# HGRN mixing with the tokens divided by two in seven levels instead of by four in three and a half

## The chip, the cores and the metric

The kernel runs on one core of a Trainium2 chip. The metric is the device time of one execution in microseconds (us). Before the change the median of three runs is 2312.23 us (2312.05 to 2313.69).

## What is computed

The model is a two-layer trunk on 256 tokens of width 2048, all in float32. Layer 0 mixes tokens with HGRN2, a gated linear recurrence with 16 heads of key width 128; layer 1 with a causal gate (gMLP). Each is followed by a gated ConvFFN, and each of the four steps ends in a residual and a layer norm. The change concerns the token mixing of HGRN2 alone:

```python
proj = x @ w_in
q, f, i, g = jnp.split(proj, ...)
q = silu(q); v = i
log_forget = logaddexp(log(lb), log1p(-lb) + log_sigmoid(f))
k = (1.0 - lb) * sigmoid(-f)
...
cum = jnp.cumsum(lf_c, axis=2)
rel = cum[:, :, :, None, :] - cum[:, :, None, :, :]
decay = jnp.exp(jnp.where(mask[:, :, None], rel, -jnp.inf))
scores = jnp.einsum('bhtk,bhsk,bhtsk->bhts', q_c, k_c, decay)
out = (jnp.einsum('bhts,bhsv->bhtv', scores, v_c) + ...)   # plus the carried state
...
o = o * rsqrt(mean(o * o) + RMS_EPS) * norm_g * silu(g)
return o @ w_out
```

The score of a later token t with an earlier token s is a sum over the key width of q[t] * k[s] * (product of the forget gates after s up to t).

## The kernel before

**Weights.** All weights arrive from HBM in chunks of 512 x 512 (1 MB, SyncE's queue, `fetch`). `convert` splits each into two float32r parts: `whi` by a copy on ScalarE (line 83), `wlo` by a subtraction on VectorE (line 84), in two halves. At most three chunks are held ahead.

**Products.** `block_b` (lines 149 and 156) has the weights stationary and makes an output of 512 features x 256 tokens; `block_a` (lines 113 to 115) has the activations stationary. Both feed TensorE with two float32r parts, three products for each exact one.

**HGRN.** `hgrn` runs four groups of four heads. A group is `block_b` for q, `block_b` for f, `block_a` for v, then two calls of `mix` (two heads each), then `block_b` for the gate `sg`, whose result is needed only after the mixing. The code is unrolled, and a scheduler places the instructions of each engine's queue when the program is built: what comes first in the program has priority, and what is ready earlier may be put ahead. On TensorE, products of the `sg` block are thus placed among those of `mix`. An engine takes its own queue strictly in that order.

**The mixing of two heads** (`mix`). The key feature is on the partition; `q`, `f`, `k1` hold 2 heads x 256 tokens = 512 elements a partition. For each head and each half of 128 tokens (index `th`, four of them; `own(th)` is its slice) the scores [s, t] are a 128 x 128 tile. They are collected in `sc`, and after that multiplied with `v`. The steps:

- `Q = q * f` (line 524); `pd`: four products of `k` and `q`, whose diagonals go to `sc` by a predicated copy (528 to 530).
- Three levels with b = 1, 4, 16 (lines 531 to 573). The tokens are divided in groups of four segments of b. `K` carries the gates from s to the end of its segment, `Q` those from the start of t's segment, `T` the product of a whole segment. For a pair of segments at distance 1, 2 or 3 the gates of the segments between are missing, so a tile `W` of 192 columns for each `th` holds three versions of `Q`: a copy on ScalarE (538) and two multiplications on VectorE (539, 540). Four products `K` x `W` (544) go into two tiles `pl` in PSUM, and six predicated copies (553) with `mask[b]` put the three distances into `sc`. Five small multiplications make `G` and the next `T` (through the helper `mul`, whose instructions all stand at line 559). New `Q` and `K` for segments four times as long come from two copies on ScalarE (567, 570) and four multiplications on VectorE.
- A last level with b = 64, written out: four products of 128 columns (577) and one predicated copy with `upper` (578).
- The cross term between the two halves, `pc` (592), and the output `pout` (600 to 602).

The PSUM tiles of all these (`pd`, `pl`, `pc`, `pout`) share a pool, `misc`, of two slots. `Q`, `K` and `T` have two slots each, `W` and `G` one. `masks` (on GpSimd) builds the masks once at the start.

A float32 product that isn't split (all of those in `mix`) appears in the trace as two passes, each with its own weight load. Matmul records are on the engine PE, weight loads on PEld.

Of the kernel before, what the change touches and what calls it, by code (L numbers as in the profile page):

```python
# [8 lines left out]
F32 = mybir.dt.float32  # L9
F32R = mybir.dt.float32r  # L10
U32 = mybir.dt.uint32
AF = mybir.ActivationFunctionType
ALU = mybir.AluOpType
PSUM = bass.MemoryType.PSUM

P = 128
S = 256
# [11 lines left out]
LEVELS = (1, 4, 16)  # L29
# [6 lines left out]
class Trunk:  # L36
    """Activations that feed products are kept as an exact sum of two float32r parts,
    feature on the partition, [P, k, part, token]; weights are split the same way as
    they arrive, and a product is hi*hi + hi*lo + lo*hi."""
# [21 lines left out]
    # ---------------------------------------------------------------- weights  # L61
# [37 lines left out]
    # ---------------------------------------------------------------- products  # L99
    def block_a(self, act, ka, w, k0, nch, c0, evac, staggered=False, halves=False):  # L100
        """out[token, c0:c0+NB]; act is stationary."""
# [38 lines left out]
    def block_b(self, act, w, nch, c0, evac, halves=False):  # L140
        """out[c0 + feature, token] in four tiles, [P, main | rest, token]; the weights
        are stationary."""
# [47 lines left out]
    def gather(self, pool, ps, out):  # L190
        """out = main + rest of a tile of block_b."""
        nc = self.nc
        r = pool.tile([P, S], F32, tag="rest", name="rest")
        nc.scalar.copy(r, ps[:, 1, :])  # L194
        nc.vector.tensor_tensor(out, ps[:, 0, :], r, ALU.add)

    def split(self, out, k, src):
        """out[:, k] = the two parts of src [P, token]."""
        nc = self.nc
        nc.scalar.copy(out[:, k, 0, :], src)  # L200
        nc.vector.tensor_tensor(
            out[:, k, 1, :], src, out[:, k, 0, :].bitcast(F32), ALU.subtract
        )

    # ---------------------------------------------------------------- constants
# [13 lines left out]
    def load_vectors(self, rows_sb):  # L219
        """Per-feature vectors as columns: feature k*P + p of row r at [p, base + k]."""  # L220
# [50 lines left out]
    def bounds(self, h1):  # L271
        """lb = softmax over the rows of lb_logits, row 0, and 1 - lb."""
# [15 lines left out]
    # ---------------------------------------------------------------- layouts  # L288
    def turn(self, t, k0, n=4, g=None, b=None):
        """X[:, k0 : k0 + n, :, half t] from the columns of z[half t], with x -> g*x + b."""  # L290
# [20 lines left out]
    # ---------------------------------------------------------------- layer norm  # L311
# [15 lines left out]
    def norm(self, name, l, store=None):  # L327
        """Layer norm of z, half by half as its last product arrives. With store, the
        result goes there; without, it goes to X, and z holds it once residual() has run."""
# [43 lines left out]
    def add_z(self, c, first=False, last=False):  # L373
        """evac of block_a: z[:, t, NB columns c] gains the product, the first time as
        ALPHA * z + product."""
        nc = self.nc

        def evac(t, ps):
            with self.tc.high_priority() if last else nullcontext():
                step(t, ps)  # L380

        def step(t, ps):
            zz = self.z[:, t, c * NB : (c + 1) * NB]
            if first:
                nc.vector.scalar_tensor_tensor(zz, zz, ALPHA, ps, ALU.mult, ALU.add)
            else:
                nc.vector.tensor_tensor(zz, zz, ps, ALU.add)  # L387
            if last:
                nc.vector.bn_stats(self.stats[t][:, c, :], zz)
                if c == 3:  # L390
                    self.after_stats(t)

        return evac

    # ---------------------------------------------------------------- HGRN2
# [12 lines left out]
    def masks(self):  # L408
        """mask[b][s, (group, i, r)] = 1 where row s lies in segment i of that group of four
        segments of b rows."""  # L410
        nc, cp = self.nc, self.cp
        self.mask = {}
        for b in LEVELS:
            n = P // 4 // b
            m = cp.tile([P, n, 3, b], F32, name=f"mask{b}")
            nc.gpsimd.memset(m, 1.0)
            nc.gpsimd.affine_select(
                out=m, in_=m, pattern=[[-4 * b, n], [-b, 3], [0, b]], compare_op=ALU.is_ge,
# [3 lines left out]
                out=m, in_=m, pattern=[[4 * b, n], [b, 3], [0, b]], compare_op=ALU.is_ge,  # L422
# [3 lines left out]
        self.upper = cp.tile([P, 1], F32, name="upper")  # L426
        nc.gpsimd.memset(self.upper, 1.0)
        nc.gpsimd.affine_select(
            out=self.upper, in_=self.upper, pattern=[[0, 1]], compare_op=ALU.is_ge,
            fill=0.0, base=P // 2 - 1, channel_multiplier=-1,  # L430
        )
# [82 lines left out]
    def mix(self, q, f, k1, v, sc, o, ss, lp, h1):  # L514
        """Two heads. The decay between s < t is a product of forget gates; it is taken as
        (gates from s to the end of its segment) * (gates of the segments between) *
        (gates from the start of t's segment), at the one level of a division of the tokens
        by four at which s and t part. Q and K carry the outer two."""
        nc = self.nc
        flat = lambda x: x.rearrange("p h n -> p (h n)")  # L520
        own = lambda th: slice((th % 2 * 2 + th // 2) * P, (th % 2 * 2 + th // 2 + 1) * P)
        K, T = flat(k1), flat(f)
        Q = lp.tile([P, 2 * S], F32, tag="Q", name="Q")
        nc.vector.tensor_tensor(Q, flat(q), T, ALU.mult)
# [6 lines left out]
        for b in LEVELS:  # L531
            n = 2 * S // (4 * b)
            seg = lambda x: x.rearrange("p (n i r) -> p n i r", i=4, r=b)
            row = lambda x: x.unsqueeze(3).to_broadcast([*x.shape, b])
            Qv, Kv, Tv = seg(Q), seg(K), T.rearrange("p (n i) -> p n i", i=4)
            W = lp.tile([P, 4, 192], F32, tag="W", name="W", bufs=1)
            Wv = W.rearrange("p x (n i r) -> p (x n) i r", i=6, r=b)
            nc.scalar.copy(Wv[:, :, 0:3, :], Qv[:, :, 1:4, :])
            nc.vector.tensor_tensor(Wv[:, :, 3:5, :], Qv[:, :, 2:4, :], row(Tv[:, :, 1:3]), ALU.mult)
            nc.vector.tensor_tensor(Wv[:, :, 5:6, :], Wv[:, :, 4:5, :], row(Tv[:, :, 1:2]), ALU.mult)  # L540
            for t in range(2):
                pl = self.misc.tile([P, 2, 192], F32, tag="m", name="pl")
                for h in range(2):
                    nc.tensor.matmul(  # L544
                        pl[:, h, :], K[:, own(2 * t + h)], W[:, 2 * h + t, :], start=True, stop=True
                    )
                at = 0
                for d in (1, 2, 3):
                    w = (4 - d) * b
                    dst = sc[:, t].rearrange("p h (n x) -> p h n x", x=4 * b)[:, :, :, d * b :]  # L550
                    src = pl.rearrange("p h (n x) -> p h n x", x=6 * b)[:, :, :, at : at + w]
                    mk = self.mask[b].bitcast(U32)[:, :, 0 : 4 - d, :].rearrange("p n i r -> p n (i r)")
                    nc.vector.copy_predicated(  # L553
                        dst, mk.unsqueeze(1).to_broadcast([P, 2, P // 4 // b, w]), src
                    )
                    at += w
            G = lp.tile([P, P, 4], F32, tag="G", name="G", bufs=1)[:, :n, :]
            Tn = lp.tile([P, P], F32, tag="T", name="T")[:, :n]
            mul = lambda out, x, y: nc.vector.tensor_tensor(out, x, y, ALU.mult)  # L559
            mul(G[:, :, 0], Tv[:, :, 0], Tv[:, :, 1])  # L560
            mul(G[:, :, 1], G[:, :, 0], Tv[:, :, 2])
            mul(G[:, :, 3], Tv[:, :, 2], Tv[:, :, 3])
            mul(G[:, :, 2], G[:, :, 3], Tv[:, :, 1])
            mul(Tn, G[:, :, 0], G[:, :, 3])
            Qn = lp.tile([P, 2 * S], F32, tag="Q", name="Q")
            Kn = lp.tile([P, 2 * S], F32, tag="K", name="K")
            nc.scalar.copy(seg(Qn)[:, :, 0, :], Qv[:, :, 0, :])
            mul(seg(Qn)[:, :, 1:2, :], Qv[:, :, 1:2, :], row(Tv[:, :, 0:1]))
            mul(seg(Qn)[:, :, 2:4, :], Qv[:, :, 2:4, :], row(G[:, :, 0:2]))
            nc.scalar.copy(seg(Kn)[:, :, 3, :], Kv[:, :, 3, :])  # L570
            mul(seg(Kn)[:, :, 2:3, :], Kv[:, :, 2:3, :], row(Tv[:, :, 3:4]))
            mul(seg(Kn)[:, :, 0:2, :], Kv[:, :, 0:2, :], row(G[:, :, 2:4]))
            Q, K, T = Qn, Kn, Tn
        b = P // 2
        pl = self.misc.tile([P, 4, P], F32, tag="m", name="pl")
        for th in range(4):
            nc.tensor.matmul(pl[:, th, :], K[:, own(th)], Q[:, own(th)], start=True, stop=True)  # L577
        nc.vector.copy_predicated(
            scv[:, :, b:], self.upper.bitcast(U32).unsqueeze(2).to_broadcast([P, 4, b]), pl[:, :, b:]
        )  # L580
# [38 lines left out]
    def staggered_pass(self, act, ka, w, k0):  # L619
        """The last CK k-tiles of all four column blocks, half t = 0 first."""  # L620
# [15 lines left out]
    # ---------------------------------------------------------------- gMLP  # L636
# [90 lines left out]
    # ---------------------------------------------------------------- ConvFFN  # L727
# [128 lines left out]
```

## Time and profile before

| what | value |
|---|---|
| device time, median of 3 runs | 2312.23 us |
| span of the profiled execution, first to last instruction | 2310.0 us |
| mean granted TensorE clock | 0.998 |
| VectorE / ScalarE busy, whole span | 1499.2 / 1090.2 us |
| first products of the four groups' mixing (`pd`) at | 83.5, 190.3, 297.2, 404.0 us |
| HBM, read and written | 185 GB/s over the span |

The device time includes what lies around the span. Busy time of an engine counts the stretches in which at least one of its instructions was in flight; TensorE's are pipelined, so a record is longer than the distance between two of them. In a chain of waits, on the other hand, the length of a piece is the time for which it held the end back. The chain of work is followed back from the last instruction, and names for each stretch of time the one engine and line that everything behind it had to wait for.

### The profile page before, as it was taken

How to read it: one execution, taken by the hardware profiler on the slowest of the kernel's cores; microseconds unless marked ns; L12 is line 12 of the kernel's file. 1: busy time of each engine (PE TensorE's matmuls, PEld its weight loads, DVE VectorE, ACT ScalarE, POOL GpSimd, SP SyncE). 2: the span in 40 equal slices, each digit the busy share in tenths (PEclk: the TensorE clock that was granted, in tenths of full speed). 3: DMA queues.
4: the chain of work that ended last, by engine and by line, in shares of the span. 5: the costliest groups of instructions: out<-in, count | busy, mean ns of one | idle time of the engine just before them, and what ended most of it. 6: DMA issues, size and time to landing. Idle time of an engine off the chain costs nothing.

```text
span 2310.0 us, 30477 instructions
## 1 busy us (share of the span) xinstructions
PE 2287.9 (99%) x12141; PEld 1956.5 (85%) x12141; DVE 1499.2 (65%) x2407; ACT 1090.2 (47%) x1642; POOL 43.3 (2%) x86
## 2 busy tenths in 40 slices
PE   8999999999999999999999999999999999999998
PEld 7888888888888888888888888888888888888886
DVE  5868786857765666456665776566765566466656
ACT  5565555536443444334443645445443444344442
POOL 2000000000000000000000000000000000000000
PEclk9999999999999999999999999999999999999999
DMA  7454535464466555555555676655565555555553
GB/s 257 129 185 137 187 134 185 146 234 158 170 214 218 188 183 182 200 182 187 191 189 182 201 223 192 214 181 178 189 228 182 193 183 189 194 189 183 182 198 112
DMA packets 214046, 430.05 MB, mean 186 GB/s; under 512 B 7544, under 2 KB 8336, under 8 KB 213904
## 3 DMA queue, kind: packets, MB, share of 16 engines
q1 hardware_dynamic: 209536, 415.26, 53.2%
q0 software_dynamic: 4368, 12.85, 1.9%
q8 instruction: 95, 1.56, 0.3%
q14 instruction: 47, 0.39, 0.0%
HBM read 425.98 MB, written 2.10 MB: 185 GB/s over the span
## 4 chain that ended last, share of the span: by engine, by line
PE 96%; DVE 2%; DMA 1%; ACT 0%; SPq 0%; issue 0%; DVEq 0%; ACTq 0%
PE pb L149 38%; PE pb L156 19%; PE pa L115 12%; PE pa L114 12%; PE pa L113 12%; PE pl L544 1%; DMA z<-in_x_dram 1%; DVE wlo L84 0%; PE pt L295 0%; DVE scores L553 0%; PE pg L710 0%; PE pa L632 0%; PE pa L633 0%; PE pa L631 0%; PE pl L577 0%; DVE K L559 0%
## 5 line engine op out<-in xcount | busy, mean ns | idle before, releaser
L84 DVE TENSOR_TENSOR wlo<-raw,whi 128x1024 fp32r<-128x1024 f32 (+1 forms) x786 | 929.4, 1218 | 683.5 <-ACT whi L83 675.6
L149 PE MATMUL pb<-X,whi 128*128 128x512 f32 (+1 forms) x3960 | 1348.8, 391 | 1.9 <-DVE X L307 1.9
L83 ACT CAST whi<-raw 128x1024 fp32r<-128x1024 f32 (+1 forms) x786 | 789.5, 1047 | 911.9 <-PE pb L149 435.3
L156 PE MATMUL pb<-X,wlo 128*128 128x256 f32 x3840 | 1054.5, 282 | 0.0
L149 PEld LDWEIGHTS pb<-X,whi 128*128 128x128 f32 x3960 | 726.5, 188 | 166.9 <-DVE X L307 2.4
L156 PEld LDWEIGHTS pb<-X,wlo 128*128 128x128 f32 x3840 | 713.1, 188 | 4.9
L115 PE MATMUL pa<-whi,Y 128*128 128x512 f32 x928 | 365.1, 393 | 0.0
L114 PE MATMUL pa<-wlo,Y 128*128 128x512 f32 x928 | 364.6, 393 | 0.0
L113 PE MATMUL pa<-whi,Y 128*128 128x512 f32 x928 | 361.3, 389 | 0.0
L114 PEld LDWEIGHTS pa<-wlo,Y 128*128 128x128 f32 x928 | 174.3, 188 | 39.6
L113 PEld LDWEIGHTS pa<-whi,Y 128*128 128x128 f32 x928 | 174.2, 188 | 38.8
L115 PEld LDWEIGHTS pa<-whi,Y 128*128 128x128 f32 x928 | 174.5, 188 | 35.3
L194 ACT COPY rest<-pb 128x256 f32<-128x256 f32 x240 | 87.3, 369 | 115.6 <-PE pb L149 112.3
L115 PE MATMUL pa<-whi,X 128*128 128x512 f32 x256 | 100.7, 393 | 0.0
L113 PE MATMUL pa<-whi,X 128*128 128x512 f32 x256 | 100.3, 392 | 0.0
L114 PE MATMUL pa<-wlo,X 128*128 128x512 f32 x256 | 100.2, 392 | 0.0
L761 DVE SCALAR_TENSOR_TENSOR act<-a,cols,act 128x254 f32<-128x254 f32 (+1 forms) x176 | 73.1, 477 | 0.0
L114 PEld LDWEIGHTS pa<-wlo,X 128*128 128x128 f32 x256 | 48.1, 188 | 10.8
L115 PEld LDWEIGHTS pa<-whi,X 128*128 128x128 f32 x256 | 48.1, 188 | 10.2
L113 PEld LDWEIGHTS pa<-whi,X 128*128 128x128 f32 x256 | 48.1, 188 | 10.0
L387 DVE TENSOR_TENSOR z<-z,pa 128x512 f32<-128x512 f32 x40 | 27.4, 684 | 34.3 <-PE pa L115 30.1
L553 DVE COPY_PREDICATED scores<-mask,pl 128x192 f32<-128x192 uint32 (+2 forms) x144 | 40.9, 354 | 2.0 <-PE pl L544 1.8
(161 smaller groups left out, 1082.0 us busy)
## 6 DMA issues: line engine op xcount, KB each, us to landing
raw<-in_ffn_w_up_dram SPq DMA_DIRECT2D x176, 1024.0 KB, 4.9
raw<-in_ffn_w_down_dram SPq DMA_DIRECT2D x88, 1024.0 KB, 5.1
raw<-in_hg_w_in_dram SPq DMA_DIRECT2D x63, 1024.0 KB, 5.1
raw<-in_sg_w_in_dram SPq DMA_DIRECT2D x32, 1024.0 KB, 5.5
raw<-in_hg_w_out_dram SPq DMA_DIRECT2D x16, 1024.0 KB, 5.1
raw<-in_sg_w_out_dram SPq DMA_DIRECT2D x16, 1024.0 KB, 5.1
g<-in_ln_g_dram POOLq DMA_DIRECT2D x16, 256.0 KB, 5.9
b<-in_ln_b_dram POOLq DMA_DIRECT2D x16, 256.0 KB, 8.7
```

What stands on the lines that cost most here:

```text
L83: nc.scalar.copy(hi[:, s, :], raw[:, s, :])
L84: self.last_lo = nc.vector.tensor_tensor(lo[:, s, :], raw[:, s, :], hi[:, s, :].bitcast(F32), ALU.subtract)
L113: nc.tensor.matmul(ps[t], xh, hi[:, kk, :], start=n[t] == 0, stop=False)
L114: nc.tensor.matmul(ps[t], xh, lo[:, kk, :], start=False, stop=False)
L115: nc.tensor.matmul(ps[t], xl, hi[:, kk, :], start=False, stop=last)
L149: nc.tensor.matmul(ps[j][:, :, s], ch[0][:, k % CK, c], act[:, k, :, s], start=start and k == 0, stop=k == last, skip_group_check=halves,)
L156: nc.tensor.matmul(ps[j][:, 1, :], ch[1][:, k % CK, c], act[:, k, 0, :], start=False, stop=False, skip_group_check=halves,)
L194: nc.scalar.copy(r, ps[:, 1, :])
L387: nc.vector.tensor_tensor(zz, zz, ps, ALU.add)
L544: nc.tensor.matmul(pl[:, h, :], K[:, own(2 * t + h)], W[:, 2 * h + t, :], start=True, stop=True)
L553: nc.vector.copy_predicated(dst, mk.unsqueeze(1).to_broadcast([P, 2, P // 4 // b, w]), src)
L761: nc.vector.scalar_tensor_tensor(cv[:, d:], x[:, : S - d], self.c(("cw", l, 2 - d), f), cv[:, d:], ALU.mult, ALU.add,)
```

## The change

The division is by two throughout: `LEVELS = (1, 2, 4, 8, 16, 32, 64)`. At a level, only the pairs (first segment s, second segment t) of each group of two are new, so no gates lie between, and the product takes the second segments of `Q` in place: 64 columns for each `th`, every other run of b. `W`, `G` and the written-out last level go; one PSUM tile and one predicated copy serve a level. In between, `Q`, `K` and `T` are renewed six times. The masks have 64 columns each. Comments and blank lines go too.

```diff
-LEVELS = (1, 4, 16)
+LEVELS = (1, 2, 4, 8, 16, 32, 64)
...
         for b in LEVELS:
-            n = P // 4 // b
-            m = cp.tile([P, n, 3, b], F32, name=f"mask{b}")
+            n = P // 2 // b
+            m = cp.tile([P, n, b], F32, name=f"mask{b}")
...
+        mul = lambda out, x, y: nc.vector.tensor_tensor(out, x, y, ALU.mult)
...
         for b in LEVELS:
-            n = 2 * S // (4 * b)
-            seg = lambda x: x.rearrange("p (n i r) -> p n i r", i=4, r=b)
-            row = lambda x: x.unsqueeze(3).to_broadcast([*x.shape, b])
-            Qv, Kv, Tv = seg(Q), seg(K), T.rearrange("p (n i) -> p n i", i=4)
-            W = lp.tile([P, 4, 192], F32, tag="W", name="W", bufs=1)
-            Wv = W.rearrange("p x (n i r) -> p (x n) i r", i=6, r=b)
-            nc.scalar.copy(Wv[:, :, 0:3, :], Qv[:, :, 1:4, :])
-            nc.vector.tensor_tensor(Wv[:, :, 3:5, :], Qv[:, :, 2:4, :], row(Tv[:, :, 1:3]), ALU.mult)
-            nc.vector.tensor_tensor(Wv[:, :, 5:6, :], Wv[:, :, 4:5, :], row(Tv[:, :, 1:2]), ALU.mult)
-            for t in range(2):
-                pl = self.misc.tile([P, 2, 192], F32, tag="m", name="pl")
-                for h in range(2):
-                    nc.tensor.matmul(
-                        pl[:, h, :], K[:, own(2 * t + h)], W[:, 2 * h + t, :], start=True, stop=True
-                    )
-                at = 0
-                for d in (1, 2, 3):
...
-                    nc.vector.copy_predicated(
-                        dst, mk.unsqueeze(1).to_broadcast([P, 2, P // 4 // b, w]), src
-                    )
-                    at += w
-            G = lp.tile([P, P, 4], F32, tag="G", name="G", bufs=1)[:, :n, :]
...
+            n = S // b
+            seg = lambda x: x.rearrange("p (n i r) -> p n i r", i=2, r=b)
+            row = lambda x: x.unsqueeze(2).to_broadcast([P, n, b])
+            Qv, Kv, Tv = seg(Q), seg(K), T.rearrange("p (n i) -> p n i", i=2)
+            pl = self.misc.tile([P, 4, P // 2], F32, tag="m", name="pl")
+            for th in range(4):
+                at = own(th).start // (2 * b)
+                nc.tensor.matmul(
+                    pl[:, th, :], K[:, own(th)], Qv[:, at : at + P // 2 // b, 1, :],
+                    start=True, stop=True,
+                )
+            nc.vector.copy_predicated(
+                scv.rearrange("p a (n i r) -> p a n i r", i=2, r=b)[:, :, :, 1, :],
+                self.mask[b].bitcast(U32).unsqueeze(1).to_broadcast([P, 4, P // 2 // b, b]),
+                pl.rearrange("p a (n r) -> p a n r", r=b),
+            )
+            if b == P // 2:
+                break
             Qn = lp.tile([P, 2 * S], F32, tag="Q", name="Q")
             Kn = lp.tile([P, 2 * S], F32, tag="K", name="K")
+            Tn = lp.tile([P, S], F32, tag="T", name="T")[:, :n]
             nc.scalar.copy(seg(Qn)[:, :, 0, :], Qv[:, :, 0, :])
-            mul(seg(Qn)[:, :, 1:2, :], Qv[:, :, 1:2, :], row(Tv[:, :, 0:1]))
-            mul(seg(Qn)[:, :, 2:4, :], Qv[:, :, 2:4, :], row(G[:, :, 0:2]))
-            nc.scalar.copy(seg(Kn)[:, :, 3, :], Kv[:, :, 3, :])
-            mul(seg(Kn)[:, :, 2:3, :], Kv[:, :, 2:3, :], row(Tv[:, :, 3:4]))
-            mul(seg(Kn)[:, :, 0:2, :], Kv[:, :, 0:2, :], row(G[:, :, 2:4]))
+            mul(seg(Qn)[:, :, 1, :], Qv[:, :, 1, :], row(Tv[:, :, 0]))
+            nc.scalar.copy(seg(Kn)[:, :, 1, :], Kv[:, :, 1, :])
+            mul(seg(Kn)[:, :, 0, :], Kv[:, :, 0, :], row(Tv[:, :, 1]))
+            mul(Tn, Tv[:, :, 0], Tv[:, :, 1])
             Q, K, T = Qn, Kn, Tn
         b = P // 2
-        pl = self.misc.tile([P, 4, P], F32, tag="m", name="pl")
-        for th in range(4):
-            nc.tensor.matmul(pl[:, th, :], K[:, own(th)], Q[:, own(th)], start=True, stop=True)
-        nc.vector.copy_predicated(
-            scv[:, :, b:], self.upper.bitcast(U32).unsqueeze(2).to_broadcast([P, 4, b]), pl[:, :, b:]
-        )
```

More of the change, by code (lines that the diff above doesn't have):

```diff
@@ L413, in masks @@
         for b in LEVELS:
-            n = P // 4 // b
-            m = cp.tile([P, n, 3, b], F32, name=f"mask{b}")
+            n = P // 2 // b
+            m = cp.tile([P, n, b], F32, name=f"mask{b}")
             nc.gpsimd.memset(m, 1.0)
             nc.gpsimd.affine_select(
-                out=m, in_=m, pattern=[[-4 * b, n], [-b, 3], [0, b]], compare_op=ALU.is_ge,
+                out=m, in_=m, pattern=[[-2 * b, n], [0, b]], compare_op=ALU.is_ge,
                 fill=0.0, base=0, channel_multiplier=1,
@@ L421, in masks @@
             nc.gpsimd.affine_select(
-                out=m, in_=m, pattern=[[4 * b, n], [b, 3], [0, b]], compare_op=ALU.is_ge,
+                out=m, in_=m, pattern=[[2 * b, n], [0, b]], compare_op=ALU.is_ge,
                 fill=0.0, base=b - 1, channel_multiplier=-1,
@@ L425, in masks @@
             self.mask[b] = m
[L426 to L430, printed above, removed]
-        )
     def hgrn(self):
@@ L521, in mix @@
         own = lambda th: slice((th % 2 * 2 + th // 2) * P, (th % 2 * 2 + th // 2 + 1) * P)
+        mul = lambda out, x, y: nc.vector.tensor_tensor(out, x, y, ALU.mult)
         K, T = flat(k1), flat(f)
         Q = lp.tile([P, 2 * S], F32, tag="Q", name="Q")
-        nc.vector.tensor_tensor(Q, flat(q), T, ALU.mult)
+        mul(Q, flat(q), T)
         scv = sc[:, 0:2].rearrange("p t h n -> p (t h) n")
@@ L540, in mix @@
-            nc.vector.tensor_tensor(Wv[:, :, 5:6, :], Wv[:, :, 4:5, :], row(Tv[:, :, 1:2]), ALU.mult)
-            for t in range(2):
-                pl = self.misc.tile([P, 2, 192], F32, tag="m", name="pl")
-                for h in range(2):
-                    nc.tensor.matmul(
-                        pl[:, h, :], K[:, own(2 * t + h)], W[:, 2 * h + t, :], start=True, stop=True
-                    )
-                at = 0
-                for d in (1, 2, 3):
[L549 to L553, printed above, removed]
-                        dst, mk.unsqueeze(1).to_broadcast([P, 2, P // 4 // b, w]), src
-                    )
-                    at += w
@@ L557, in mix @@
-            G = lp.tile([P, P, 4], F32, tag="G", name="G", bufs=1)[:, :n, :]
[L558 to L564, printed above, removed]
+            n = S // b
@@ L573, in mix @@
+            nc.scalar.copy(seg(Kn)[:, :, 1, :], Kv[:, :, 1, :])
+            mul(seg(Kn)[:, :, 0, :], Kv[:, :, 0, :], row(Tv[:, :, 1]))
+            mul(Tn, Tv[:, :, 0], Tv[:, :, 1])
             Q, K, T = Qn, Kn, Tn
         b = P // 2
-        pl = self.misc.tile([P, 4, P], F32, tag="m", name="pl")
-        for th in range(4):
-            nc.tensor.matmul(pl[:, th, :], K[:, own(th)], Q[:, own(th)], start=True, stop=True)
-        nc.vector.copy_predicated(
-            scv[:, :, b:], self.upper.bitcast(U32).unsqueeze(2).to_broadcast([P, 4, b]), pl[:, :, b:]
-        )
```

## The prediction

> **What bounds the kernel now.** I read the page first: busy shares, then the chain that ended last.
>
> ```profile
> span 2310.0 us, 30477 instructions
> ...
> PE 2287.9 (99%) x12141; PEld 1956.5 (85%) x12141; DVE 1499.2 (65%) x2407; ACT 1090.2 (47%) x1642; POOL 43.3 (2%) x86
> ...
> PE 96%; DVE 2%; DMA 1%; ACT 0%; SPq 0%; issue 0%; DVEq 0%; ACTq 0%
> ```
>
> TensorE is busy 99% of the span and carries 96% of the chain. An average hides stages, so the second view was the busy time by stretch, for the time in which the mixing of one group runs and for the whole group.
>
> ```profile
> 190.00:218.00 28.00, 27.81 (x176) 25.04 (x175) 26.24 (x91) 14.69 (x34) 0.00 (x0) 1.00 0.21 71
> 190.00:297.00 107.00, 106.81 (x603) 92.90 (x602) 79.82 (x189) 58.60 (x111) 0.00 (x0) 1.00 0.49 158
> ```
>
> The columns after the length are PE, PEld, DVE, ACT and POOL. In the mixing stretch VectorE is nearly full (26.24 of 28.00 us), and still TensorE idles for only 0.19 us of it. The third view, the chain in order of time, says why: between mixing products TensorE runs products of the block for the gate `sg` (line 149 with `whi`, line 156 with `wlo`), which need nothing of the mixing. So what the change is worth is the time that its own products occupy TensorE, plus the waits inside the mixing that the filling leaves open. Neither VectorE nor ScalarE is the limit. The granted clock is 1.00 throughout.
>
> Rows of that chain give the price of a mixing product; columns are start, length, work.
>
> ```profile
> 190.34 0.89 PE pd L528 x8
> ...
> 196.39 0.23 PE pb L149
> 196.62 0.12 PE pb L156
> 196.74 0.88 PE pl L544 x4
> ...
> 208.16 0.92 PE pl L544 x4
> ...
> 211.02 1.54 PE pl L544 x8
> ...
> 214.54 1.30 PE pl L544 x8
> ...
> 217.01 0.89 PE pl L577 x8
> 217.90 0.45 PE pc L592 x4
> ...
> 297.16 0.89 PE pd L528 x8
> ```
>
> Four float32 products appear as eight instructions: each is two passes with a weight load of its own. A pass of 128 columns costs 0.89/8 = 0.111 us, one of 192 columns 1.30/8 = 0.1625 us when it waits for nothing. The period of a group is 297.16 - 190.34 = 106.82 us.
>
> **The change, part by part.** There are eight mixings (four groups, two halves).
>
> *Products removed and added.* Each mixing loses 3 levels x 4 products of 192 columns (24 passes) and the last level's 4 products of 128 (8 passes): 24 x 0.1625 + 8 x 0.111 = 3.90 + 0.89 = 4.79 us. It gains 7 levels x 4 products of 64 columns: 56 passes. Columns streamed fall from 2816 to 1792, but weight loads rise from 32 to 56. The rest (`pd`, `pc`, `pout`) stays. So everything hangs on what a 64-column pass costs, which this trace doesn't show: its narrowest plain float32 pass has 128.
>
> From below: the step from 128 to 192 columns costs (0.1625 - 0.111)/64 = 0.80 ns a column, so a pass that only streams takes 0.111 - 0.051 = 0.060 us. From above: a 128-column pass with its load takes 0.111 us, and a narrower one has no reason to take more. To choose, I looked at how loads and products interlock.
>
> ```profile
> 217.63 0.28 PE L577 MATMUL pl<-Q,K 128*128 128x128 f32 x1
> ...
> 217.74 0.28 PE L592 MATMUL pc<-Q,K 128*128 128x128 f32 x1
> ...
> 217.63 0.30 PEld L592 LDWEIGHTS pc<-Q,K 128*128 128x128 f32 x2
> ...
> 208.16 0.19 PEld L544 LDWEIGHTS pl<-W,k 128*128 128x128 f32 x1 [0.42 <-DVE scores L530]
> 208.16 0.43 PE L544 MATMUL pl<-W,k 128*128 128x192 f32 x1
> ...
> L544 PE MATMUL pl<-W,k x64: 326/326/431, 84.2 to 422.4; 128*128 128x192 f32 x64
> ```
>
> The first load of `pc` starts at 217.63, the moment the pass before it starts, and its own pass starts 0.11 us later: one load runs ahead, not two. At 208.16 TensorE had been idle, so nothing hid the load; that pass reads 431 ns where the usual one reads 326 (minimum/median/maximum in the last row). The 105 ns between are the uncovered load. Transposes give the contrast:
>
> ```profile
> 38.94 0.32 PE L264 MATMUL pv<-ident,rows 120*128 120x120 f32 x1 [0.47 <-DVE cols L265]
> ...
> 39.57 0.24 PE L264 MATMUL pv<-ident,rows 88*128 88x88 f32 x1
> ...
> L503 PEld LDWEIGHTS po<-ident,o 128*128 128x128 f32 x32 | 3.8, 140 | 0.4
> ...
> L544 PEld LDWEIGHTS pl<-W,K 128*128 128x128 f32 x128 | 20.7, 190 | 3.1 <-issue 2.5
> ```
>
> From 88 to 120 columns a transpose should grow by 32 x 0.80 = 26 ns; the uncovered one grew by 80, so its load costs about 54 ns, and its load records are 140 ns long against 190. The 50 ns between 190 and 140 and those between 105 and 54 are the same: a plain float32 load occupies the weight path about 105 ns, a transpose's half of that. The load of `K` in the changed kernel is the plain kind, 128 columns. A 64-column stream of some 53 ns can't hide 105 ns, so a pass is paced by its load. **I take 0.111 us**, the upper bound and the row nearest to it: 56 x 0.111 = 6.23 us, against 4.79, **+1.44 us a mixing, 8 x 1.44 = +11.5 us**. The break-even pass is 4.79/56 = 0.0855 us. The product now reads `Q` in steps (every other run of b columns) where `W` was dense; no row shows a stepped moving operand, but even twice the stream, 0.107 us, lies under the load, and none would gain.
>
> The Trainium skill ("TensorE: Matmul & The Clock Gate", section "LDWEIGHTS") speaks against this change: a load takes its column count over 1.2 ns, whatever the rows, hence 107 ns for `K`. By that rule alone the estimate is 56 x 0.107 = 5.99 us, +9.6 us in all; the trace's 105 ns agrees.
>
> *Waits inside the mixing.* At 208.16 four passes took 0.92 instead of 0.65 (0.27 late), at 211.02 eight took 1.54 instead of 1.30 (0.24 late), after a short idle: some 0.6 us a mixing, 4.8 us in all. The number of `pl` tiles is the same (3 x 2 + 1 = 7 before, 7 after), and the two PSUM slots rotate as before. Level 1 now needs only `Q` and `k`, not the copy and two multiplications behind `W`; but there are seven hand-overs of `Q` and `K` in a row where there were four. Bounds: all gone, -4.8 us; doubled, +4.8 us. I take 0, the mean.
>
> *VectorE, ScalarE, GpSimd.* Work on them changes, all beside TensorE.
>
> ```profile
> L553 DVE COPY_PREDICATED scores<-mask,pl 128x192 f32<-128x192 uint32 x48 | 18.5, 397 | 1.9 <-PE pl L544 1.8
> L553 DVE COPY_PREDICATED scores<-mask,pl 128x128 f32<-128x128 uint32 x48 | 16.4, 358 | 0.1
> L553 DVE COPY_PREDICATED scores<-mask,pl 128x64 f32<-128x64 uint32 x48 | 13.7, 308 | 0.0
> L538 ACT COPY W<-Q 128x384 f32<-128x384 f32 x24 | 13.1, 544 | 18.4 <-PE pl L544 14.6 <-DVE Q L524 3.2
> L559 DVE TENSOR_TENSOR Q<-Q,G 128x256 f32<-128x256 f32 x24 | 10.1, 421 | 0.0
> L578 DVE COPY_PREDICATED scores<-upper,pl 128x256 f32<-128x256 uint32 x8 | 3.5, 438 | 0.0
> L559 DVE TENSOR_TENSOR T<-G 128x8 f32<-128x8 f32 x8 | 1.3, 168 | 0.0
> ...
> L194 ACT COPY rest<-pb 128x256 f32<-128x256 f32 x240 | 87.3, 369 | 115.6 <-PE pb L149 112.3
> ```
>
> Predicated copies: 18.5 + 16.4 + 13.7 + 3.5 = 52.1 us go, 56 of 256 elements at 438 ns come, 24.5 us. `W`'s and `G`'s multiplications go; the twelve 256-element multiplications of `Q` and `K` cost 12 x 0.421 = 5.1 us a mixing, and T's six add about 1.6 (the first as 0.421, the last as 0.168). A level then holds VectorE for about 0.438 + 2 x 0.421 + 0.27 = 1.5 us by record lengths, less as records overlap. ScalarE loses the 24 copies of `W` and 48 smaller ones and gains 96 of 256 elements at about 0.369 us, 35 us in all over eight mixings, while it stands at 14.69 of 28.00. GpSimd builds seven masks instead of three; its last work of this kind ends at 21 us and the first mixing starts at 83, rows below. All this I cost at nothing: the gate block hides it. If that cover were gone, each of the seven levels would show its wait (below). No DMA is added or moved, so the queues are as before.
>
> ```profile
> 20.34 0.74 POOL L445 MEMSET scores<- 128x768 f32 x1
> ...
> 83.48 0.89 PE pd L528 x8
> ```
>
> *Sum.* +11.5 us. The profile's span is 2310.0; the median of the runs is 2312.23, so 2.2 us lie around it, unchanged. **2312.2 + 11.5 = 2323.7 us.** About 0.2%, 4.6 us, is what measuring this kernel can tell from no change.
>
> **The rivals.**
>
> *The pass is paced by its stream (faster).* If the load of a narrow pass overlaps more than one pass ahead, a pass costs 0.060 us: 56 x 0.060 = 3.36 us, -1.43 a mixing, 2312.2 - 11.4 = 2300.8 us. It decides wherever a pass takes under 0.0855 us. For it: fewer columns, and TensorE is the bound. Against it: loads one ahead only, and the 105 ns. The same page of the Trainium skill, section "Back-to-back issue gap", gives N/2.4 + 2.5 ns, which for 64 columns taken twice is an estimate of 56 ns and 2298.9 us; the page itself says that this gap leaves out the loads, and no row here shows plain passes below 0.111 us.
>
> *In between (no change).* If only part of the 105 ns occupies the path and the rest is a latency that a run of loads overlaps, a pass takes 0.075 to 0.095 us around the break-even: -4.7 to +4.2 us, about 2312. For it: a load record is 190 ns and overlaps its neighbours. Against it: in a run of 128-column passes, load, stream and pace coincide at 0.11.
>
> *The seven hand-overs show.* `Q` and `K` pass through VectorE and ScalarE seven times in series; if each level makes TensorE wait as at 208.16, 0.27 us: 7 x 8 x 0.27 = 15.1 us on top, 2338.8 us. For it: the level chain is longer and VectorE is full in this stretch. Against it: VectorE's load falls, and slower passes give it more time per level.
>
> **How the numbers follow.** My forecast, paced by the load with waits between gone and doubled (2318.9 to 2328.5), gets 0.70; paced by the stream 0.13; in between 0.09; the hand-overs 0.08. The range takes in the in-between case's centre and half of the hand-over case: 2309 to 2339, leaving out the stream case and some tails, about 0.18. Faster: 0.13. Same: 0.11, the in-between case and the low edge of the forecast. Slower: 0.76.
>
> **What would show each step.** Right: the passes of `pl` follow each other by about 0.11 us within a run of eight (0.89 us), not 0.48; a group's period grows by about 2.9 us to 109.7, in the mixing stretch alone; VectorE's busy time falls by some tens of us with no gain. If eight passes take under 0.68 us, the load step is wrong. If they take 0.89 and the time still falls, the waits were larger than I read them. If idle time of TensorE or late passes with a VectorE releaser appear at each level, the hand-overs are the cause. Outside the four mixing stretches nothing should move.

## The result and the profile after

| | before | changed |
|---|---|---|
| device time, median | 2312.41 us (4 runs, 2312.05 to 2313.69) | 2327.68 us (4 runs, 2327.39 to 2328.12) |
| ratio to before, 95% interval | | 1.0065 (1.0052 to 1.0077) |
| span of the profiled execution | 2310.0 us | 2326.1 us |
| VectorE busy | 1499.2 us | 1466.8 us |

Slower by 15.3 us, where 11.5 were forecast. The page of the changed kernel looks as before, with less work on VectorE:

```profile
span 2326.1 us, 30800 instructions
...
PE 2304.2 (99%) x12333; PEld 1965.5 (84%) x12333; DVE 1466.8 (63%) x2191; ACT 1100.2 (47%) x1666; POOL 43.9 (2%) x96
...
PE 95%; DVE 2%; issue 1%; DMA 1%; ACT 0%; SPq 0%; POOL 0%; DVEq 0%; POOLq 0%; ACTq 0%
```

The chain in order of time shows the new products. Columns are start, length, work; the first rows are the second group's first mixing.

```profile
192.83 0.89 PE pd L523 x8
193.72 0.84 PE pl L534 x8
194.56 0.29 PE pb L149
194.85 0.12 PE pb L156
194.97 0.23 PE pb L149
195.20 0.84 PE pl L534 x8
196.04 0.17 PE pb L156
196.21 0.84 PE pl L534 x8
...
301.40 0.89 PE pd L523 x8
...
409.98 0.89 PE pd L523 x8
```

A run of eight 64-column passes takes 0.84 us, and the first `pb` pass behind it lasts 0.05 us longer than usual (0.17 for 0.12, 0.29 for 0.23). The weight loads in the timeline say why:

```profile
195.93 0.98 PEld L534 LDWEIGHTS pl<-Q,K 128*128 128x128 f32 x8
196.83 0.19 PEld L149 LDWEIGHTS pb<-X,whi 128*128 128x128 f32 x1
```

From the first load of a run to the load behind it are 0.90 us, eight loads at 0.112. By the ends of the records, the first pass of a run, whose load has run ahead, adds 0.056 us (the median of the 56 runs), and each of the other seven ends 0.112 us after the one before: 0.056 + 7 x 0.112 = 0.84. The 0.05 us behind the run are what the last narrow stream could not cover of the next load. So a run costs 0.84 + 0.05 = 0.89 us in all, 0.111 a pass. A group's period is 301.40 - 192.83 = 108.57 us, 1.75 more than before; four groups make 7.0 us. The fourth group's mixing starts at 409.98 instead of 403.99.

So the mixing stretches hold less than half of the loss. From the fourth mixing's start to the end of the span it is 2326.1 - 409.98 = 1916.1 us against 2310.0 - 403.99 = 1906.0: 10.1 us, of which 1.75 at most is that mixing. Some 8 us lie in stages that the change doesn't touch. Busy time by stretch finds them. Behind the length stands TensorE's busy time with its count of passes; the first row of each fence lies in the first FFN's downward product (`block_a` only), the second in its upward product (`block_b` only). Before:

```profile
920.00:1000.00 80.00, 80.00 (x352) 65.63 (x351) 40.62 (x41) 30.15 (x32) 0.00 (x0) 1.00 0.57 192
1030.00:1180.00 150.00, 150.00 (x852) 130.39 (x851) 96.41 (x147) 71.01 (x107) 0.00 (x0) 1.00 0.54 187
```

After, the same work some 10 us later:

```profile
930.00:1010.00 80.00, 80.00 (x344) 64.29 (x343) 39.17 (x38) 28.67 (x31) 0.00 (x0) 1.00 0.55 184
1040.00:1190.00 150.00, 150.00 (x859) 130.81 (x858) 96.89 (x149) 71.40 (x107) 0.00 (x0) 1.00 0.57 189
```

The same full busy time and the same clock of 1.00, but 344 passes of `block_a` where there were 352, and 859 of `block_b` where there were 852. I took the paces from the starts in the timeline, over 12 passes of `block_a` and over 16 pairs (`whi`, `wlo`) of `block_b`: **228.9 to 234.3 ns** for a pass of 512 columns, **353.2 to 350.2 ns** for a pair, all along the kernel. With 3648 such passes of `block_a` and 3840 pairs that is 3648 x 5.4 - 3840 x 3.0 ns = 19.7 - 11.5 = +8.2 us. Together with 7.0 us in the mixing this is 15.2 of the measured 15.3.

What could reach those products? The masks. Seven of 64 columns take 7 x 256 = 1792 bytes a partition, three of 96 and `upper` took 3 x 384 + 32 = 1184. The weight tiles lie behind them, and moved by 608 bytes; `X` and `Y`, the other operand of these products, lie ahead and stayed.

### The profile page after: what moved, and what is told of

Read it like the earlier page. It is cut to its first block, busy times and chain, and to the rows that moved or that the text cites. A ratio compares the mean times of both kernels' runs of the same rounds, so it can differ in the third digit from the quotient of the medians.

```text
span 2326.1 us, 30800 instructions
## 1 busy us (share of the span) xinstructions
PE 2304.2 (99%) x12333; PEld 1965.5 (84%) x12333; DVE 1466.8 (63%) x2191; ACT 1100.2 (47%) x1666; POOL 43.9 (2%) x96
## 4 chain that ended last, share of the span: by engine, by line
PE 95%; DVE 2%; issue 1%; DMA 1%; ACT 0%; SPq 0%; POOL 0%; DVEq 0%; POOLq 0%; ACTq 0%
PE pb L149 37%; PE pb L156 19%; PE pa L113 12%; PE pa L114 12%; PE pa L115 12%; PE pl L534 2%; DVE wlo L84 1%; DMA z<-in_x_dram 1%; PE pt L295 0%; PE pd L523 0%; PE pg L684 0%; DMA bb<-in_sg_ln_b_dram 0%; PE pa L607 0%; PE pa L606 0%; PE pa L605 0%
## 5 line engine op out<-in xcount | busy, mean ns | idle before, releaser
L113 PE MATMUL pa<-whi,Y 128*128 128x512 f32 x928 | 368.2, 397 | 0.0
L115 PE MATMUL pa<-whi,Y 128*128 128x512 f32 x928 | 367.9, 396 | 0.0
L114 PEld LDWEIGHTS pa<-wlo,X 128*128 128x128 f32 x256 | 48.2, 188 | 11.5
L534 PEld LDWEIGHTS pl<-Q,K 128*128 128x128 f32 x384 | 48.8, 191 | 2.1
```

The costliest lines, as they stand in the source:

```text
L113: nc.tensor.matmul(ps[t], xh, hi[:, kk, :], start=n[t] == 0, stop=False)
L114: nc.tensor.matmul(ps[t], xh, lo[:, kk, :], start=False, stop=False)
L115: nc.tensor.matmul(ps[t], xl, hi[:, kk, :], start=False, stop=last)
L534: nc.tensor.matmul(pl[:, th, :], K[:, own(th)], Qv[:, at : at + P // 2 // b, 1, :], start=True, stop=True,)
```

## The experiments

Each ran beside the kernel before on the same chip. Edits that only move tiles lengthen a tile or add an unused one. Paces are taken as above, medians and intervals as in the first table.

| run | us | ratio to before (95%) | block_a pass, ns | block_b pair, ns |
|---|---|---|---|---|
| before | 2312.41 | | 228.9 | 353.2 |
| changed | 2327.68 | 1.0065 (1.0052 to 1.0077) | 234.3 | 350.2 |
| e1, changed, weights +32 bytes | 2330.72 | 1.008 (1.0065 to 1.0095) | 233.2 | 353, some 349 |
| e2, before, weights +32 bytes | 2305.64 | 0.997 (0.9959 to 0.9981) | 233.1 | 346.9 |
| e3, changed, loads of 64 columns | 2322.68 | 1.0045 (1.003 to 1.006) | 234.3 | 350.2 |
| e4, changed, 128 columns moved | 2335.57 | 1.01 (1.0085 to 1.0116) | 234.3 | 350.3 |
| e5, before at the changed kernel's addresses | 2320.50 | 1.0035 (1.0022 to 1.0048) | 234.3 | 350.2 |
| e6, changed at the addresses of before | 2319.44 | 1.0029 (1.0018 to 1.0041) | 228.9 | 353.1 |
| e7, before, tiles behind the weights +32 bytes | 2312.48 | 0.9999 (0.999 to 1.0009) | 229 | 353 |
| e8, before, weights placed by use | 2316.76 | 1.0019 (1.001 to 1.0028) | 229, 232, 233 in turn | 344 to 353 |
| e9, before, `Y` and weights +32 bytes | 2293.36 | 0.9917 (0.9901 to 0.9933) | 228.9 on `Y`, 233.3 on `X` | 346.9 |
| e10, before, `X`, `Y` and weights +32 bytes | 2312.42 | 0.9999 (0.9989 to 1.0009) | 228.9 | 353.1 |

**What paces a narrow pass: e3 and e4.** e3 halves the columns of each load, and with them the partitions of the output, and leaves the moving side alone:

```diff
-                    pl[:, th, :], K[:, own(th)], Qv[:, at : at + P // 2 // b, 1, :],
+                    pl[: P // 2, th, :], K[:, own(th)][:, : P // 2], Qv[:, at : at + P // 2 // b, 1, :],
```

> The changed kernel with products that load only the first 64 columns of K for each half of 128 tokens (scores of the other 64 earlier tokens are left out; the predicated copies cover 64 partitions). The count of products and their 64 moving columns stay. Theory load: a pass is paced by its weight load, which halves with its columns, so eight passes of pl take about 0.44 to 0.48 us instead of 0.84, and 448 passes save 448 x 0.047 = 21 us against the changed kernel, to about 2307 us. Rival, a pass of 64 columns costs 0.105 us because of its stepped moving operand or a floor of its own: no change, 2327.7 us.

The group of the loads by form (busy time, mean ns of one), the chain and the timeline of the loads in e3:

```profile
L534 PEld LDWEIGHTS pl<-Q,K 128*64 128x64 f32 x384 | 25.9, 137 | 11.4 <-issue 5.9 <-ACT K L550 2.0 <-ACT whi L83 1.0
```

```profile
207.95 0.61 PE pl L534 x8
208.56 0.32 PE pb L156
```

```profile
209.30 0.19 PEld L149 LDWEIGHTS pb<-X,whi 128*128 128x128 f32 x1
209.74 0.54 PEld L534 LDWEIGHTS pl<-Q,K 128*64 128x64 f32 x8 [0.25 <-issue]
210.34 0.19 PEld L156 LDWEIGHTS pb<-X,wlo 128*128 128x128 f32 x1
```

and the same group in the changed kernel:

```profile
L534 PEld LDWEIGHTS pl<-Q,K 128*128 128x128 f32 x384 | 48.8, 191 | 2.1
```

A load record shrinks from 191 to 137 ns, and the eight loads of a run follow each other by 0.058 us ((0.54 - 0.137)/7) where they took 0.112, with the same moving side. So the load set the pace. The Trainium skill ("TensorE: Matmul & The Clock Gate", section "LDWEIGHTS") gives columns over 1.2 ns for a load, 53 ns less for half of them; this trace agrees, with 54. Its section "Back-to-back issue gap" gives, with 64 columns taken twice, an estimated 56 ns for a pass, and says itself that this leaves out the loads. The trace agrees: in the changed kernel the first pass of a run, whose load has run ahead, adds 0.056 us, and the others, which wait for theirs, 0.112.

But the run saves only 5.0 us of the 21 I had put down. The rows show where the rest went: at a change of width the load no longer runs ahead. The first narrow load starts only with its own pass, at 209.74, where the 512-column pass before it started at 209.42; the first wide load starts 0.14 us after the last narrow pass (210.34 against 210.20), where in the changed kernel it is 0.05. All 56 runs of e3 are like this. So a run takes 0.61 us, not 8 x 0.058 = 0.46, and the product behind it 0.32 where it took 0.17: run and successor together fall from 1.01 to 0.93 us, 56 x 0.08 = 4.5 us. I put this down to the change of width, but no run tests that by itself.

e4 keeps the loads and doubles the stream, now dense:

```diff
-                    pl[:, th, :], K[:, own(th)], Qv[:, at : at + P // 2 // b, 1, :],
+                    pl[:, th, :], K[:, own(th)], Q[:, own(th)],
```

> The changed kernel with products over all 128 columns of Q, dense, of which the predicated copy reads the same half; the result is the same. The loads are the same, the stream doubles. Theory load: the stream of 128 columns (107 ns) only just exceeds the load, eight passes take 0.89 instead of 0.84 us, 448 x 0.006 = 2.7 us more than the changed kernel, about 2330 us. Rival, paced by the stream at 0.80 ns a column: 448 x 0.051 = 23 us more, about 2351 us. Rival, the stepped read costs: the dense operand is faster or equal, 2327 us or less.

It is 7.9 us slower than the changed kernel, where the load theory had 2.7 and the stream 23. Its chain, and the loads of one run:

```profile
322.55 1.13 PE pl L533 x8
324.03 1.13 PE pl L533 x8
325.39 0.89 PE pl L533 x8
326.63 0.93 PE pl L533 x8
```

```profile
326.40 0.97 PEld L533 LDWEIGHTS pl<-Q,K 128*128 128x128 f32 x8
327.29 0.19 PEld L156 LDWEIGHTS pb<-X,wlo 128*128 128x128 f32 x1
```

Twice the columns don't slow the passes: loads and passes follow each other by 0.111 us ((327.29 - 326.40)/8), as in the changed kernel. A run that waits for nothing takes 0.89 us, and the product behind it its usual 0.12, so run and successor cost the same 1.01 us as before; the 2.7 us of my expectation counted the 0.84 without the 0.05 behind it. The rival in which the stream sets the pace is out. The 7.9 us lie in late first passes, like those of the runs of 1.13 us: 36 of the 56 runs have a first pass that adds 0.14 us or more, up to 0.42, where in the changed kernel none adds more than 0.11. The scheduler also placed the products otherwise: twelve runs of e4 stand right behind another run, without a product of the gate block between them, and none in the changed kernel. What each late pass waits for I didn't separate. Nor does the stepped read cost anything in a run: dense or stepped, the pace is that of the load.

**Where the other 8 us come from: e1, e2, e5, e6, e7.** The weight tiles and all that lies behind them move when the last tile of constants grows; n is 8 (32 bytes) in e1 and e2, 152 (608 bytes) in e5:

```diff
-        self.lb = cp.tile([P, 2, NK], F32, name="lb")
+        lb = cp.tile([P, 2 * NK + n], F32, name="lb")
+        self.lb = lb[:, : 2 * NK].rearrange("p (r k) -> p r k", r=2)
```

> The changed kernel with 32 bytes more behind the masks, so that the weight tiles and all that lies behind them start at a multiple of 64 bytes again, as in the kernel before (the smaller W and G don't matter for this, the larger masks do). Theory placement: block_a's passes of 512 columns go back from 234.3 to 228.9 ns (3648 of them, -19.6 us), block_b's pairs from 350.0 back to 353.2 ns (3840, +12 us); together about -7.5 us against the changed kernel, ratio to the kernel before near 1.003. Rival, the pace differs for another reason (the chip, or the order of work): both paces stay as in the changed kernel and the ratio stays near 1.0065.

> The kernel before with 32 bytes more behind the constants, so that the weight tiles and all that lies behind them start 32 bytes past a multiple of 64, as in the changed kernel; nothing else differs. Theory placement: block_a's pass 234.3 instead of 228.9 ns, block_b's pair 350.0 instead of 353.2, the mixing untouched: +7.5 us, ratio about 1.003. Rival, not the placement: ratio 1.000 and the paces of the kernel before.

Both fail, and in sign: e1 got slower by 3.0 us instead of faster by 7.5, and with 32 bytes the kernel before gets *faster* by 6.6 us. That it moves at all, with every instruction as it was, shows that the place counts and that the remainder by 64 isn't the rule. Windows of e2 as above:

```profile
918.00:998.00 80.00, 80.00 (x345) 64.34 (x344) 39.04 (x38) 28.53 (x30) 0.00 (x0) 1.00 0.54 184
1028.00:1178.00 150.00, 150.00 (x867) 132.03 (x867) 96.22 (x147) 71.80 (x107) 0.00 (x0) 1.00 0.57 190
```

`block_a` loses as in the changed kernel (345 passes), `block_b` gains far more (867): 3648 x 4.2 - 3840 x 6.3 ns = -8.9 us, somewhat more than the 6.6 measured. So I dropped the rule and tested for the place itself: e5 gives the kernel before the changed kernel's addresses, e6 the changed kernel those of before (its masks go to the pool of the HGRN stage, and `lb` is lengthened until the weights lie where they lay).

> The kernel before with 608 bytes more behind the constants, so that the weight tiles and all that lies behind them have exactly the addresses of the changed kernel; instructions as before. Theory placement (the paces of the split products follow from where their operands lie, though not from the remainder by 64 alone, as the first four runs showed): block_a's pass 234.3 ns and block_b's pair 350.1 ns, as in the changed kernel, 3648 x 5.4 - 3840 x 3.0 ns = +8.2 us, 2320.5 us; the rest to 2327.7, some 7.2 us, is then the mixing. Rival, the paces come from the order of the mixing's instructions: paces as before, 2312.3 us.

> The changed kernel with its masks in the pool that ends with the HGRN stage and the constants padded so that the weight tiles lie exactly where they lie in the kernel before. Theory placement: 228.9 ns and 353.2 ns, 2327.7 - 8.2 = 2319.5 us, which is the price of the mixing alone, +7.2 us. Rival, order of instructions: 234.3 and 350.1 ns stay, 2327.7 us.

Both came out within 0.1 us. Windows of e5, then of e6:

```profile
925.00:1005.00 80.00, 80.00 (x343) 64.29 (x343) 36.90 (x34) 28.34 (x29) 0.00 (x0) 1.00 0.57 188
1033.00:1183.00 150.00, 150.00 (x859) 130.86 (x858) 96.53 (x148) 71.12 (x107) 0.00 (x0) 1.00 0.57 188
```

```profile
926.00:1006.00 80.00, 80.00 (x352) 65.69 (x351) 40.94 (x44) 31.33 (x35) 0.00 (x0) 1.00 0.58 197
1038.00:1188.00 150.00, 150.00 (x851) 130.39 (x850) 96.08 (x146) 70.67 (x106) 0.00 (x0) 1.00 0.56 186
```

The counts go with the addresses, 343 to 344 and 859 or 352 and 851 to 852, whichever mixing the kernel has. The four kernels make a square:

| | addresses of before | addresses of the changed kernel | difference: place |
|---|---|---|---|
| mixing by four | 2312.56 (23 runs) | 2320.50 | +7.9 |
| mixing by two | 2319.44 | 2327.68 | +8.2 |
| difference: mixing | +6.9 | +7.2 | |

The two effects add.

> The kernel before with 32 bytes of an otherwise unused tile behind the weight tiles: they stay where they were, the activations' temporaries behind them move. Theory that the weight tiles' own place counts: paces 228.9 and 353.2 ns, 2312.3 us. Rival, the place of the temporaries (written and read by VectorE and ScalarE beside the products) counts: paces change by some ns as in the run with 32 bytes ahead of the weights, 2305 to 2321 us.

e7 puts an unused tile between the weights and the rest; it is the kernel before, 2312.48 us. So a shift of the temporaries by 32 bytes doesn't count.

**What of the place counts: e8, e9, e10.** e8 makes `whi` and `wlo` 64 bytes longer and starts the data of `block_b`'s chunks 32 bytes into them.

> The kernel before, each whi and wlo 64 bytes longer: a chunk for block_a starts at a multiple of 64 bytes, one for block_b 32 bytes later. The slots so differ in their remainder by 2048 (1984, 0, 64 for whi, 128, 192, 256 for wlo). If the pace follows the remainder by 64 for block_b (346.9 or 350.1 ns at 32 against 353.2 at 0) and block_a keeps 228.9: 2312.3 - 3840 x 3 to 6.3 ns = 2288 to 2301 us. If each slot has its own pace, chunks of one block differ in threes. If the pace is set by more than the weights' place, block_a moves too, to 233 ns: up to 2316 us.

The gain didn't come: 1.0019. What it shows is the third case: in `block_a` successive chunks run at 229, 232 and 233 ns, over and over, as the three slots with their different places take turns. The pace belongs to the place of a chunk, not to a stage.

e9 and e10 move both operands. The edit is an unused tile of 32 bytes, in e9 between `X` and `Y`, in e10 ahead of `X`:

```diff
         self.X = cp.tile([P, NK, 2, S], F32R, name="X")
+        pad = cp.tile([P, 8], F32, name="pad")
+        nc.gpsimd.memset(pad, 0.0)
         self.Y = cp.tile([P, NK, 2, S], F32R, name="Y")
```

> The kernel before with 32 bytes between X and Y: Y (the stationary side of most of block_a) and the weights move by 32 bytes, X stays. Theory that the distance between the two operands of a pass counts: block_a on Y keeps 228.9 ns, as before (Y and weights moved together), block_b on X has 346.9 ns as in the run with 32 bytes ahead of the weights: 2305.6 - 2880 x 4.2 ns = 2293.5 us. Rival, each operand's own place counts: block_a stays at 233.1 ns or finds a third pace; with 233.1 it is 2305.6 us.

> The kernel before with 32 bytes ahead of X: X, Y and the weights all move by 32 bytes. Theory of the distance: all paces as before, 228.9 and 353.2 ns, 2312.4 us. Rival, the own place of the weights counts: 233.1 and 346.9 ns, 2305.6 us.

The theory of the distance was right to 0.2 us in both. Windows of e9:

```profile
916.00:996.00 80.00, 80.00 (x351) 65.64 (x350) 38.49 (x37) 28.59 (x29) 0.00 (x0) 1.00 0.57 189
1024.00:1174.00 150.00, 150.00 (x868) 132.07 (x867) 95.98 (x147) 71.70 (x108) 0.00 (x0) 1.00 0.57 190
```

`block_a` on `Y` is back at 351 passes, since `Y` and the weights moved together; `block_b`, whose moving side `X` stayed, has 868, as e2 had 867. `block_a` on `X`, which the weights moved away from, runs at 233.3 ns, as in e2. With all three moved (e10) every pace is that of before, though the weights lie just where they lie in e2. It is the distance between the stationary and the moving operand that counts. **e9 beats both kernels: 2293.36 us, ratio 0.9917 (0.9901 to 0.9933) to the kernel before**, by one unused tile of 32 bytes. Which distances are good wasn't mapped; e1's gave 233 ns, and pairs at 353 or 349 by whole blocks, which I can't explain.

## Why the prediction was right, and where it was wrong

The measured 2327.7 us lie in the range, 4.0 us above the forecast, and partly by luck: the mixing cost 4 to 5 us less than I had put down, and a term I hadn't put down cost 8.

**A pass paced by its load: right, in mechanism and in size.** The rival in which the stream sets the pace (0.060 us, 2300.8 us) is out: seven of the eight passes of a run follow by 0.112 us in all seven levels; e3 moved this with the load, and e4, with twice the stream, did not. With the 0.05 us behind it a run of eight costs 0.89 us, the 0.111 a pass that I took, so the term is 8 x 1.44 = +11.5 us as put down. The load itself takes 0.112 us in a run, a little more than the 105 ns that I read off a single uncovered one.

**Waits inside the mixing: taken as 0, they went.** Without the effect of the place (e6 against before) the mixing costs 6.9 us, 4.6 less than its passes alone: nearly the whole of my bound "all gone, -4.8 us". This term of the sum was mis-sized. By the ends of the records, the `pl` passes with what they delay behind them take 43.6 us before (38.3 at full pace, 5.3 late) and 50.3 us in the changed kernel (49.8 at 0.111, 0.5 late). I had read the waits of before off two rows of TensorE and passed over where the chain runs: between 197.62 and 208.16 it is on VectorE almost all the way. Its last rows there:

```profile
206.18 0.64 DVE Q L559 x2
206.82 0.64 DVE K L559 x2
207.46 0.66 DVE scores L530
208.11 0.04 issue
208.16 0.92 PE pl L544 x4
```

In the changed kernel the chain stays on TensorE through all the mixing stretches. The rival of the seven hand-overs is out: TensorE doesn't idle any more in a group (107.00 of 107.00 us, where it was 106.81), and no first pass of a run is more than some 0.05 us late.

```profile
190.00:297.00 107.00, 107.00 (x643) 94.26 (x642) 70.27 (x135) 60.17 (x117) 0.00 (x0) 1.00 0.48 154
```

The same row shows VectorE at 70.27 us for 79.82 and ScalarE at 60.17 for 58.60. I had costed this work at nothing; less of it on VectorE may well be what ended the waits, but no run separates it from the new order of the products. e4, with as much of it as the changed kernel, has late passes again.

**"Outside the four mixing stretches nothing should move": wrong.** This step failed. I counted what the edits do to engines and queues, GpSimd's seven masks among them, but not that larger masks push every weight tile 608 bytes further. That cost 7.9 to 8.2 us, as much as the change itself. The group period should have shown it: forecast 109.7 us, measured 108.57, too short a step for a total that was longer. The sum came out near because the two errors, about -4.6 and +8.2 us, had opposite signs.

## What to carry to other kernels

On a bound TensorE, count weight loads beside streamed columns: here a pass cost 0.11 us with 64 columns as with 128, so below 128 columns cutting saved nothing, and every further product cost a load. When a kernel moves in stages that the change doesn't touch, compare the counts of the same instruction in equal windows, then the addresses: a constant tile that grows shifts all that lies behind it. An edit's own price is known only at equal addresses, and a tile of a few bytes may be worth more than the edit.

## What the runs showed that I had not expected

Passes of the split products, back to back, with the same clock and the same instructions, run at 228.9, 233.1 or 234.3 ns (512 columns) and pairs at 346.9, 350.2 or 353.2 ns, as the distance between the stationary and the moving operand in SBUF changes by 32 or 608 bytes; moving both by 32 bytes changes nothing. Why the distance counts stays open. Over the whole kernel this is worth 19.2 us between the kernel before and e9.
